# First layer's feed-forward output by seven block products in three passes; second layer's modulation multiplied by GpSimd and summed by ScalarE

## The chip, the cores and the metric

The kernel runs on one core of a Trainium2 chip. The profile names the engines PE (TensorE's matmuls), PEld (its weight loads), DVE (VectorE), ACT (ScalarE), POOL (GpSimd) and SP (SyncE, which here issues DMAs alone). The metric is the device time of one execution in microseconds, the median of several runs.

## The reference

Two passes of a two-layer transformer share all weights: 128 context tokens and 512 latent tokens, 640 columns in all, of model width 1024. Every sub-layer is modulated by a condition (shift, scale and gate, one set for the context tokens and one for the latent ones), and each layer ends with a SwiGLU feed-forward of inner width 2816:

```python
def ada_modulation(cond, w_mod, b_mod):
    m = jax.nn.silu(cond) @ w_mod + b_mod
    return jnp.split(m, 6, axis=-1)

def swiglu(h, w_in, w_out):
    gate, up = jnp.split(h @ w_in, 2, axis=-1)
    return (jax.nn.silu(gate) * up) @ w_out

for l in range(DEPTH):
    sh1_p, sc1_p, g1_p, sh2_p, sc2_p, g2_p = ada_modulation(cond_ctx, w_mod[l], b_mod[l])
    ...
    xp = xp + g1_p * out_p
    hp = modulate(rms_norm(xp, norm_ffn[l]), sh2_p, sc2_p)
    xp = xp + g2_p * swiglu(hp, w_ffn_in[l], w_ffn_out[l])
```

The latent tokens (xs, hs) go the same way. Layer 0's mixer is latent attention and neighbourhood attention, layer 1's is grouped-query attention. All is float32.

## The kernel before

Activations lie with features on the 128 partitions, as 8 tiles of 128x640, in two halves of 320 columns. A float32 product is made of three matmuls (`mm3`): weight and operand are each split into a rounded high part (ACT copies it) and a low part (DVE subtracts it from the source, "split" below), and high x high, high x low and low x high are added in PSUM.

*Feed-forward input.* The first three of 22 feature blocks are plain matmuls. The 19 others, the loop blocks, use a scheme with seven half-size products in place of eight for the 2x2 blocks (gate and up) x (left and right columns): DVE makes sums of the weights (`seven`: X and W are the raw weights, Y and Z are sums), ACT and DVE split them, and PE makes seven products of 12 matmuls into the banks fg, fd and fu, with operands named q, D, C, N, E. ACT copies partial results out of PSUM (p, u), DVE adds them (up, g), ACT applies silu, DVE multiplies (sg). Both layers do this alike.

*Feed-forward output.* In layer 1 (`ffn_out_seven`) it is a seven-product scheme as well: `hidden_pair` turns each pair of blocks into seven operands (a, D, N, b, c, C, E) split by ACT and DVE and spilled to DRAM by SP (all but two pairs of eleven); the output then goes over three passes of 3, 4 and 4 pairs, in each over 4 pairs of output tiles, and reloads the operands pass by pass. In layer 0 it is direct: `hidden` splits each block once (hd), and two chunks of 9 and 13 blocks are multiplied into 8 output tiles, two halves each (fo); `residual` adds them to x on DVE. After the second chunk comes the norm of layer 1 (fn0) and its first operands (h10); half of the last two tiles is held back so that PE has work meanwhile.

*Modulation.* Layer 0's is mostly made by matmuls at the start. The remaining 48 tiles, layer 0's last gate (G2) and layer 1's first five sets, are made by `mod_side`: SP loads a 128x1024 weight tile, and DVE multiplies it with the silu of either condition (a broadcast tile cb) and sums over the row, in one instruction with an accumulated output (junk). Four tiles go in layer 0's output projection (`mixer_out`), 44 in layer 0's feed-forward, at places set by a table of counts by block and tile. Layer 1's last set is made in layer 1 the same way.

*Order.* Each engine runs its instructions in one fixed order, written down when the program is built; `after(x, f)` places what f issues behind x. A tile name with `bufs` buffers makes a writer wait until the buffer's last reader is done.

Of the kernel before, what the change touches and what calls it, by code (L numbers as in the profile page):

```python
# [45 lines left out]
FO_ORDER = list(range(FB - 3, FB)) + list(range(FB - 3))  # L46
# [5 lines left out]
def body(ctx, tc, xT, vecs, crow, wm0, wm0g1, wm0g, wm1, wA, wNV, wNA, wMK, wMV, wOA, wGQ, wGK, wGV, wOC,  # L52
         wFI, wFO, wFO1, cckvT, ckrT, cnkT, cnv, cgkT, cgv, rpbp, tabM, tabK, tabG, maskN,
# [143 lines left out]
    class Norm:  # L197
# [6 lines left out]
        def add(self, x, i, last=False):  # L204
            c0, c1 = HALF[i]
            if last:
                sq = self.alone[i] = tp.tile([P, HT], F32, tag="u", bufs=7, name=f"{self.name}sql{i}")
                S.activation(sq, x[:, c0:c1], AF.Square)
            elif self.k[i] == 0:
                S.activation(self.acc[:, c0:c1], x[:, c0:c1], AF.Square)  # L210
            else:
                sq = tp.tile([P, HT], F32, tag="u", bufs=7, name=f"{self.name}sq{self.k[i]}{i}")
                S.activation(sq, x[:, c0:c1], AF.Square)
                V.tensor_add(self.acc[:, c0:c1], self.acc[:, c0:c1], sq)
            self.k[i] += 1

# [942 lines left out]
    def mixer_out(wsrc, os_, order, xin, ml, name, nxt, pre, beside=None, early=False, hold=None):  # L1159
# [5 lines left out]
        if True:  # L1165
# [4 lines left out]
            def evac(n, c, ps):  # L1170
# [3 lines left out]
                nrm.add(x[n], c, n == KT - 1)  # L1174
# [60 lines left out]
    STAY = 3  # L1235
    FIRST, SECOND = FO_ORDER[:9], FO_ORDER[9:]

# [4 lines left out]
    def ffn_open(l):  # L1242

        ph = ExitStack()
        fk = ph.enter_context(tc.tile_pool(name=f"fk{l}", bufs=1, reuse_waits="tile"))
        dr = ph.enter_context(tc.tile_pool(name=f"dr{l}", bufs=1, space=bass.MemoryType.DRAM))
        fs = ExitStack()
        if l == 0:
            hd = [[fk.tile([P, T], F32R, name=f"hd{l}_{i}{c}") for c in "hl"] for i in range(1)]
            fp = su = fs.enter_context(tc.tile_pool(name=f"fp{l}", bufs=1, reuse_waits="tile"))  # L1250

            def scratch(name):
                a = fk.tile([P, 2 * D], F32, tag="cb", bufs=1, name=name + "32a")
                d = [fp.tile([P, 1024], F32, tag="wr", bufs=2, name=f"{name}32d{i}") for i in range(2)]
                room = [t[:, j * HT:j * HT + HT] for t, n in ((a, 6), (d[0], 3), (d[1], 3)) for j in range(n)]
                room += [tp.tile([P, HT], F32, tag="u", bufs=7, name=f"{name}32u{i}") for i in range(4)]
                return room[:KT], room[KT:]
        else:
            hd = []
            fp = ph.enter_context(tc.tile_pool(name=f"fp{l}", bufs=1, reuse_waits="tile"))  # L1260
            su = fs.enter_context(tc.tile_pool(name=f"su{l}", bufs=1, reuse_waits="tile"))

            def scratch(name):

                left, right = {}, {}
                for at, where in (((0, 4), left), ((1, 5), left), ((0, 1), right), ((2, 6), left), ((3, 7), left), ((2, 3), right)):
                    t = fk.tile([P, T], F32, tag="o", bufs=7, name=f"{name}32{'rl'[where is left]}{at[0]}")
                    for k, c in zip(at, HALF):
                        where[k] = t[:, c[0]:c[1]]
                for k in range(4, KT):  # L1270
                    right[k] = tp.tile([P, HT], F32, tag="u", bufs=7, name=f"{name}32u{k}")
                return [left[k] for k in range(KT)], [right[k] for k in range(KT)]
        w = []

        def pre():
            for i in range(2):
                w.append(unit(wFI[l, 0, i], 1024, f"wgu{l}_{i}", pool=fp))
        return ph, fk, dr, hd, fs, fp, w, (su, scratch), pre

    def seven(ru, rg, name, fp, split):  # L1280
# [3 lines left out]
        wX = split(ru, f"wX{name}")  # L1284
        t = fp.tile([P, 2, 512], F32R, tag="w4", bufs=2, name=f"wW{name}")
        wW = t[:, 0, :m], t[:, 1, :m]
        S.activation(wW[0], rg[:, m:], AF.Copy)
        V.tensor_tensor(wW[1], rg[:, m:], f(wW[0]), ALU.subtract)
        s13 = fp.tile([P, 1024], F32, tag="ws", bufs=2, name=f"s13{name}")[:, :n]
        V.tensor_tensor(s13[:, :m], rg[:, :m], rg[:, m:], ALU.add)  # L1290
        V.tensor_tensor(s13[:, m:], ru[:, :m], rg[:, :m], ALU.add)
        wY = split(s13, f"wY{name}")
        s24 = fp.tile([P, 1024], F32, tag="ws", bufs=2, name=f"s24{name}")[:, :n]
        V.tensor_tensor(s24[:, :m], s13[:, m:], rg[:, m:], ALU.add)
        V.tensor_tensor(s24[:, m:], s24[:, :m], ru[:, m:], ALU.add)
        wZ = split(s24, f"wZ{name}")
        return wX, wW, wY, wZ

    def ffn_out_seven(x, nxt, opened, ops, spilt, split, close, last):

        ph, fk, dr, hd, fs, fp, *_ = opened
        ng = gs[0][0]
        V.tensor_scalar_mul(ng, mods[1][:, G2:G2 + 8, :], -1.0)
        raws = [0]

        def raw(n, c0, m, name):
# [3 lines left out]
            nc.sync.dma_start(t, wFO1[n, :, c0:c0 + m])  # L1310
# [10 lines left out]
        def result(n, c, src, sign, end):  # L1321

            o = HALF[c][0]
            for c0, c1, i in HCOND[c]:
                V.scalar_tensor_tensor(x[n][:, c0:c1], src[:, c0 - o:c1 - o],
                                       ng[:, n, i:i + 1] if sign < 0 else mods[1][:, G2 + n, i:i + 1], x[n][:, c0:c1], ALU.mult, ALU.add)
# [848 lines left out]
```

## Time and profile before

| | us |
|---|---|
| median of 3 runs | 1471.37 (1470.99 to 1471.61) |
| the profiled execution: time | 1473.53 |
| its span, first to last instruction | 1471.2 |
| PE busy in the span | 1438.7 |
| DVE busy | 1232.6 |
| ACT busy | 781.5 |
| POOL busy | 178.5 |

Layer 0's output projection (oa) runs from about 321 to 373 us, its feed-forward input to 655, the output to 809; layer 1's attention follows, its output projection (oc) from 992, its feed-forward input from 1077 and output from 1327 to the end. A row such as `700.00:750.00 50.00, 50.00 (x343)` reads: a stretch of 50 us in which PE was busy for 50.00 us with 343 instructions. A row of the timeline gives start, duration, engine, line, operation, output <- inputs, shape. One DVE operation often ends a little after the next has started.

### The profile page before, as it was taken

Reading aid. Unit: us, or ns where it says so; the run is one execution under the profiler, and the core shown is the slowest. Engines: PE = TensorE matmul, PEld = TensorE weight load, DVE = VectorE, ACT = ScalarE, POOL = GpSimd, SP = SyncE. Lnnn points to the kernel's source line nnn. Section 1 sums busy time; section 2 is a strip of 40 time slices with the busy share of each in tenths; the row PEclk is TensorE's granted clock in tenths of the full one; section 3 lists DMA queues with packets and bytes.
Section 4 is the critical chain, followed back from the end, with each engine's and each line's share of the span. In section 5 each row is a group of like instructions: output and inputs, shape, how many; then the busy total and the mean of one; then the engine's idle time right before and its main releaser. Section 6 shows DMA issues by size and latency. Waiting matters only on the chain.

```text
span 1471.2 us, 25849 instructions
## 1 busy us (share of the span) xinstructions
PE 1438.7 (98%) x9764; PEld 1391.0 (95%) x9764; DVE 1232.6 (84%) x2353; ACT 781.5 (53%) x1531; POOL 178.5 (12%) x276
## 2 busy tenths in 40 slices
PE   5999999999999999999999999999999999999997
PEld 3989979889999999999999999989999999999997
DVE  5877768977998888965997888888899898989976
ACT  5446657863755555531223666672656555555443
POOL 0046635520000000000000122220000000000000
PEclk9999999999999999999999999999999999999999
DMA  9653451125164555568764300115245555548572
GB/s 372 218 155 125 144 164 41 44 89 184 48 218 168 171 171 175 170 235 314 238 222 146 100 31 30 46 51 176 87 167 190 178 179 180 178 141 300 180 268 72
DMA packets 82724, 234.17 MB, mean 159 GB/s; under 512 B 9256, under 2 KB 15560, under 8 KB 82216
## 3 DMA queue, kind: packets, MB, share of 16 engines
q1 hardware_dynamic: 80240, 228.12, 46.2%
q10 hardware_dynamic: 1944, 3.48, 0.7%
q8 instruction: 76, 1.25, 0.3%
q0 software_dynamic: 416, 0.93, 0.2%
q14 instruction: 48, 0.39, 0.1%
HBM read 192.82 MB, written 36.66 MB: 156 GB/s over the span
## 4 chain that ended last, share of the span: by engine, by line
PE 88%; DVE 5%; ACT 3%; DMA 2%; issue 2%; SPq 0%; DVEq 0%; ACTq 0%
PE fg L64 21%; PE fd L64 9%; PE fgo L64 5%; PE fo L64 5%; PE fu L64 4%; PE gq L64 3%; PE fdo L64 2%; PE nk L64 2%; PE gs L64 2%; PE go L64 2%; PE nq L64 1%; PE fuo L64 1%; PE gt L68 1%; PE mod L64 1%; PE gvp L64 1%
## 5 line engine op out<-in xcount | busy, mean ns | idle before, releaser
L1742 DVE SCALAR_TENSOR_TENSOR junk<-wm,cb 128x1024 bf16<-128x1024 f32 x88 | 107.4, 1220 | 6.1 <-DMA wm<-in_wm 5.0
L64 PE MATMUL gq<-h10h,wgq 128*128 128x320 f32 x256 | 65.8, 316 | 0.0
L269 POOL TENSOR_SCALAR h10h<-h10t,gs,mods 128x320 fp32r<-128x320 f32 x4 | 3.9, 991 | 429.7 <-DVE h10t L263 423.7
L1482 ACT ACTIVATE wY<-s 128x1024 fp32r<-128x1024 f32 x38 | 40.3, 1061 | 26.8 <-PE fg L64 22.5
L2010 POOL TENSOR_TENSOR xr<-xw,fn1rs 128x320 f32<-128x320 f32 x2 | 1.7, 861 | 412.8 <-ACT fn1rs L237 412.8
L1482 ACT ACTIVATE wZ<-s 128x1024 fp32r<-128x1024 f32 x38 | 40.2, 1057 | 20.0 <-PE fd L64 15.2
L1483 DVE TENSOR_TENSOR wZ<-s,wZ 128x1024 fp32r<-128x1024 f32 x38 | 46.4, 1222 | 2.1
L1483 DVE TENSOR_TENSOR wY<-s,wY 128x1024 fp32r<-128x1024 f32 x38 | 46.4, 1220 | 0.3
L64 PEld LDWEIGHTS gq<-h10h,wgq 128*128 128x128 f32 x256 | 44.9, 189 | 0.6
L1591 DVE TENSOR_TENSOR sg<-up,sg 128x640 f32<-128x640 f32 x38 | 31.3, 824 | 15.7 <-ACT sg L1590 14.6
L1590 ACT ACTIVATE sg<-fg 128x320 f32<-128x320 f32 x38 | 16.7, 439 | 48.4 <-PE fg L64 48.4
L1612 ACT ACTIVATE p<-fd 128x320 f32<-128x320 f32 x38 | 16.6, 438 | 45.9 <-PE fd L64 45.8
L64 PE MATMUL gq<-h10l,wgq 128*128 128x320 f32 x128 | 39.4, 308 | 0.0
L1947 ACT ACTIVATE gp<-gs,gb,rq 128x640 f32<-128x640 f32 (+1 forms) x40 | 31.9, 796 | 13.2 <-DVE gb L1946 11.8
L64 PE MATMUL fg<-h01E,wW 128*128 128x320 f32 x228 | 36.6, 309 | 0.9 <-DVE g L1622 0.9
L64 PE MATMUL fg<-h11N,wZ 128*128 128x320 f32 x228 | 36.7, 309 | 0.0
L64 PE MATMUL fg<-h01q,wX 128*128 128x320 f32 x228 | 36.7, 309 | 0.0
L64 PE MATMUL fu<-h11q,wX 128*128 128x320 f32 x228 | 36.6, 309 | 0.0
L64 PE MATMUL fg<-h01N,wZ 128*128 128x320 f32 x228 | 36.6, 309 | 0.0
L64 PE MATMUL fd<-h01q,wZ 128*128 128x320 f32 x228 | 36.6, 309 | 0.0
L64 PE MATMUL fd<-h11q,wZ 128*128 128x320 f32 x228 | 36.6, 309 | 0.0
L64 PE MATMUL fg<-h11q,wX 128*128 128x320 f32 x228 | 36.5, 309 | 0.0
(3412 smaller groups left out, 5299.0 us busy)
## 6 DMA issues: line engine op xcount, KB each, us to landing
wm<-in_wm SPq DMA_DIRECT2D x48, 512.0 KB, 3.8
mraw<-in_wm SPq DMA_DIRECT2D x8, 1024.0 KB, 13.2
mraw<-in_wm SPq DMA_DIRECT2D x14, 512.0 KB, 3.9
wmv<-in_wm0g SPq DMA_DIRECT2D x8, 512.0 KB, 4.0
wm<-in_wm0g SPq DMA_DIRECT2D x8, 512.0 KB, 4.6
ruo<-in_wFO SPq DMA_DIRECT2D x8, 512.0 KB, 3.7
rgo<-in_wFO SPq DMA_DIRECT2D x8, 512.0 KB, 5.7
x<-in_xT SPq DMA_DIRECT2D x8, 320.0 KB, 5.3
```

The costliest lines, as they stand in the source:

```text
L64: cls.last = nc.tensor.matmul(*a, **k)
L68: cls.last = nc.tensor.transpose(*a, **k)
L269: G.tensor_scalar(h[:, c0:c1], t, self.gsl[:, k, 0:1], self.ml[:, self.sh + k, 0:1], ALU.mult, ALU.add)
L1482: S.activation(h, src, AF.Copy)
L1483: V.tensor_tensor(w_, src, f(h), ALU.subtract)
L1590: last = S.activation(sg[:, 0:HT], g[:, :HT], AF.Silu, scale=-1.0)
L1591: V.tensor_tensor(sg, up, sg, ALU.mult)
L1612: S.activation(p5, b5[:, :HT], AF.Copy)
L1742: V.scalar_tensor_tensor(junk, raw, 1.0, cb[:, c, :], ALU.mult, ALU.mult, accum_out=mods[l][:, j0 + i, c:c + 1])
L1947: gexp[h, j] = S.activation(dst, src, AF.Exp, bias=nb, scale=rq[:, j:j + 1], accum_out=ll[:, j:j + 1])
L2010: G.tensor_tensor(x[k][:, c0:c1], root[1][k], nrm.rs[:, c0:c1], ALU.mult)
```

## The change

1. Layer 0's feed-forward output takes layer 1's form: `hidden_pair` for both layers, `ffn_out_seven` with a layer argument, three passes, the weights in one tensor in the order of the passes. Its last two output tiles (e0, e1) have an order of their own in which results go from PSUM to x directly, and the next norm's calls stand between the last products.
2. 44 modulation tiles leave DVE and SP. A `Stream` makes them in 88 units of 128x512 (first all tiles' left halves, then the right ones): POOL loads a unit and multiplies it with the two conditions in two instructions (the second in place); ACT sums each product by a copy with an accumulated output ("add-up"). The right half's sum goes to a scratch column and is added at the end of a set. `pump(anchor, n)` advances it n slots behind an ACT instruction; a unit takes two slots, and the add-ups of a unit stand in the two slots after its multiplies. Slots: 26 at the squares of the output projection, 8 in layer 0's second and third block, 5 in each of its 19 loop blocks, 5 in each of the first ten output blocks: 179 for the 178 needed. The conditions come in halves of 512 as well.
3. `seven` hands its four parts out when first asked for, and layer 0 has fewer weight buffers (2 in place of 3; one for W).

```diff
-            def __init__(self, i, n, c0):
+            def __init__(self, i, n, c0, where=None, make="XWYZ"):
...
             def copy(self, what, ps):
                 t = self.held[what] = tp.tile([P, HT], F32, tag="u", bufs=7, name=f"{what}{self.name}")
-                S.activation(t, ps[:, :HT], AF.Copy)
+                pump(S.activation(t, ps[:, :HT], AF.Copy), 1 + 2 * (what == "u2"))
...
+        if l == 0:
+            pump(None, None)
+            e0 = Block(len(PASSES) - 1, 2, c0, (wp, fp, fp), "XYZ")
+            e0.p1()
+            e0.p2()
+            prev.p4()
+            e0.make("W")
+            e1 = Block(len(PASSES) - 1, 3, c0, (wp, wp, wp), "XYZ")
+            e1.p1()
+            e0.p6(True)
+            e1.p2()
+            e0.p7_direct()
+            e1.p6(True)
+            e0.p4()
+            e1.make("W")
+            e1.p7_direct()
+            e0.p5_direct()
+            e1.p4(True)
+            e1.p5_direct()
+            nxt(x, nrm, 0, range(3))
+            e0.p3_direct()
+            nxt(x, nrm, 0, range(3, 6))
+            e1.p3_direct()
+            nxt(x, nrm, 0, range(6, KT))
...
             product(g, wX, 0, 11, True)
-            S.activation(p1, g[:, :HT], AF.Copy)
+            pump(S.activation(p1, g[:, :HT], AF.Copy), 1)
...
-            for c in range(2):
-                junk = pool.tile([P, D], mybir.dt.bfloat16, tag="junk", bufs=1, name=f"junk{l}{j0 + i}{c}")
-                V.scalar_tensor_tensor(junk, raw, 1.0, cb[:, c, :], ALU.mult, ALU.mult,
-                                       accum_out=mods[l][:, j0 + i, c:c + 1])
...
+        def fetch(self, u):
+            if u < len(self.units):
+                h, l, src, j0, i = self.units[u]
+                t = self.raws[u] = self.pool.tile([P, 512], F32, tag="mr", bufs=3, name=f"wm{h}{l}_{j0 + i}")
+                G.dma_start(t, src[i][:, 512 * h:512 * h + 512])
+
+        def multiply(self, u):
...
+                t = self.pool.tile([P, 512], F32, tag="mt", bufs=2, name=f"mt{h}{l}_{j0 + i}")
+                G.tensor_tensor(t, self.raws[u], self.cb[:, 0, :], ALU.mult)
+                G.tensor_tensor(self.raws[u], self.raws[u], self.cb[:, 1, :], ALU.mult)
+                self.prods[u] = t, self.raws.pop(u)
+
+        def add_up(self, u, c, anchor):
...
+            t = self.prods[u][c]
+            m, at = (mods[1], G2 + i) if h else (mods[l], j0 + i)
+            after(anchor, lambda: S.activation(t, t, AF.Copy, accum_out=m[:, at, c:c + 1]))
...
+                if self.slot == 0:
+                    self.fetch(0)
+                    self.fetch(1)
+                self.add_up(u - 1, odd, anchor)
+                if odd:
+                    self.fetch(u + 2)
+                else:
+                    self.multiply(u)
+                self.slot += 1
```

The order on three engines at the places that matter. First ACT in layer 0's output projection, from the fifth output tile's weights (oaw) on; oansq are squares for the norm, mt and wm the two products of a unit. Before:

```order
L175 ACTIVATE oaw_4499<-oaw4r 128x1024
L210 ACTIVATE oanacc<-xr_4322 128x320 x2
L213 ACTIVATE oansq_4340<-xr_4336 128x320
L213 ACTIVATE oansq_4348<-xr_4336 128x320
L213 ACTIVATE oansq_4392<-xr_4388 128x320
L175 ACTIVATE oaw_4572<-oaw5r 128x1024
L213 ACTIVATE oansq_4421<-xr_4388 128x320
L213 ACTIVATE oansq_4465<-xr_4461 128x320
L175 ACTIVATE oaw_4610<-oaw6r 128x1024
```

And now:

```order
L1727 ACTIVATE mt_44_4337,mods_98<-mt_44_4337 128x512
L1727 ACTIVATE wm_44_4331,mods_98<-wm_44_4331 128x512
L212 ACTIVATE oansq_4362<-xr_4358 128x320
L1727 ACTIVATE mt_45_4349,mods_98<-mt_45_4349 128x512
L1727 ACTIVATE wm_45_4333,mods_98<-wm_45_4333 128x512
L212 ACTIVATE oansq_4377<-xr_4358 128x320
L1727 ACTIVATE mt_46_4366,mods_98<-mt_46_4366 128x512
L1727 ACTIVATE wm_46_4340,mods_98<-wm_46_4340 128x512
L212 ACTIVATE oansq_4428<-xr_4424 128x320
L1727 ACTIVATE mt_47_4381,mods_98<-mt_47_4381 128x512
L174 ACTIVATE oaw_4650<-oaw5r 128x1024
L1727 ACTIVATE wm_47_4353,mods_98<-wm_47_4353 128x512
```

Seven add-ups have come ahead of the split of oaw5; the splits of oaw6 and oaw7 stand behind 12 and 16.

Second, a loop block of layer 0: ACT from the split of wX for block 10 to the split of wZ (wX, wZ, wY, wW are weights, p and u copies out of PSUM, sg silu, hd the hidden block's high part). Before:

```order
L1482 ACTIVATE wX_10_6239<-wu_10r 128x1024
L1482 ACTIVATE wZ_10_6254<-s_10_6251 128x1024
L1482 ACTIVATE wY_10_6248<-s_10_6245 128x1024
L1623 ACTIVATE sg_8_5989<-g_8_5993 128x320
L1610 ACTIVATE p_9_6126<-fg_9_6121 128x320
L1612 ACTIVATE p_9_6127<-fd_9_6122 128x320
L1590 ACTIVATE sg_8_5989<-fg_8_5985 128x320
L1287 ACTIVATE wW_10_6242<-wg_10r 128x512
L1542 ACTIVATE hd_2h<-sg_8_5989 128x640
L1616 ACTIVATE u_9_6128<-fg_9_6121 128x320
L1482 ACTIVATE wX_11_6369<-wu_11r 128x1024
```

And now:

```order
L1538 ACTIVATE wX_10_6585<-wu_10r 128x1024
L1662 ACTIVATE sg_8_6280<-g_8_6284 128x320
L1727 ACTIVATE mt_26_6332,mods_99<-mt_26_6332 128x512
L1648 ACTIVATE p_9_6453<-fg_9_6448 128x320
L1727 ACTIVATE wm_26_6255,mods_99<-wm_26_6255 128x512
L1538 ACTIVATE wY_10_6591<-s_10_6588 128x1024
L1650 ACTIVATE p_9_6454<-fd_9_6449 128x320
L1727 ACTIVATE mt_27_6426,mods_99<-mt_27_6426 128x512
L1624 ACTIVATE sg_8_6280<-fg_8_6276 128x320
L1727 ACTIVATE wm_27_6316,mods_99<-wm_27_6316 128x512
L1282 ACTIVATE wW_9_6518<-wg_9r 128x512
L1564 ACTIVATE op4a<-sg_8_6280 128x320
```

Between the same copies and splits stand add-ups, one per slot; p and u are what frees PE's banks. POOL, which had no instruction from the end of the output projection to the end of layer 0, now has in the same block:

```order
L1709 DMA wm_26_6255<-in_wm 128x512
L1709 DMA wm_27_6316<-in_wm 128x512
L1717 TENSOR_TENSOR mt_26_6332<-wm_26_6255,cbs_4335 128x512
L1718 TENSOR_TENSOR wm_26_6255<-wm_26_6255,cbs_4335 128x512
L1717 TENSOR_TENSOR mt_27_6426<-wm_27_6316,cbs_4335 128x512
L1718 TENSOR_TENSOR wm_27_6316<-wm_27_6316,cbs_4335 128x512
L1709 DMA wm_28_6383<-in_wm 128x512
```

Third, PE at the end of layer 0, up to layer 1's first key product (gk). Before, the last of the held tiles' matmuls:

```order
L64 MATMUL fo_1_71_9314<-hr_17l,wo_1_71_9343 128x320
L64 MATMUL fo_1_71_9314<-hr_17h,wo_1_71_9343 128x320
L64 MATMUL fo_1_71_9314<-hr_18h,wo_1_71_9343 128x320
L64 MATMUL fo_1_71_9314<-hr_18l,wo_1_71_9343 128x320
L64 MATMUL fo_1_71_9314<-hr_18h,wo_1_71_9343 128x320
L64 MATMUL gk0a<-h10h_9407,wgk_9538 128x320
L64 MATMUL gk0a<-h10l_9415,wgk_9538 128x320
L64 MATMUL gk0a<-h10h_9407,wgk_9538 128x320
```

And now, from the norm's first matmul (fn0p) on:

```order
L63 MATMUL fn0p_10266<-fn0acc,ones 128x320
L63 MATMUL fdo_2_2_10215<-or4c,wZo_2_2_10033 128x320 x3
L63 MATMUL fdo_2_2_10215<-or5c,wZo_2_2_10033 128x320 x3
L63 MATMUL fdo_2_2_10215<-or6c,wZo_2_2_10033 128x320
L63 MATMUL fn0p_10266<-fn0sql_10246,ones 128x320
L63 MATMUL fdo_2_2_10215<-or6c,wZo_2_2_10033 128x320 x2
L63 MATMUL fdo_2_2_10215<-or7c,wZo_2_2_10033 128x320 x3
L63 MATMUL fdo_2_3_10248<-or4c,wZo_2_3_10104 128x320 x3
L63 MATMUL fdo_2_3_10248<-or5c,wZo_2_3_10104 128x320 x3
L63 MATMUL fdo_2_3_10248<-or6c,wZo_2_3_10104 128x320 x3
L63 MATMUL fdo_2_3_10248<-or7c,wZo_2_3_10104 128x320 x3
L63 MATMUL gk0a<-h10h_10271,wgk_10371 128x320
```

Behind the norm's second matmul stand 2 + 3 + 12 = 17 matmuls of the last products before gk0a; before the change 57 of the held halves stood behind the norm's.

434 lines of the change are left out of this document (183 added, 251 removed).

## The prediction

> **What bounds the kernel now.** I read the page's engine shares and slices first, then busy time by stage, then single instructions in order of time.
>
> ```profile
> span 1471.2 us, 25849 instructions
> ...
> PE 1438.7 (98%) x9764; PEld 1391.0 (95%) x9764; DVE 1232.6 (84%) x2353; ACT 781.5 (53%) x1531; POOL 178.5 (12%) x276
> ...
> DVE  5877768977998888965997888888899898989976
> ...
> POOL 0046635520000000000000122220000000000000
> ```
>
> PE is full, DVE is near full, and POOL does next to nothing from the tenth slice to the twenty-second, where layer 0's feed-forward runs. The busy times of that part, and of the same stages of layer 1, which already have the changed form (columns: us, then busy us of PE, PEld, DVE, ACT, POOL, clock, DMA share, GB/s):
>
> ```profile
> 321.00:365.00 44.00, 44.00 (x303) 44.00 (x302) 31.27 (x63) 14.37 (x23) 0.00 (x0) 1.00 0.65 219
> 476.96:526.22 49.26, 49.26 (x339) 49.26 (x338) 44.62 (x66) 25.89 (x40) 0.00 (x0) 1.00 0.52 177
> 700.00:750.00 50.00, 50.00 (x343) 50.00 (x342) 48.28 (x86) 11.42 (x15) 0.00 (x0) 1.00 0.72 234
> 1148.86:1198.12 49.26, 49.26 (x339) 49.26 (x338) 44.37 (x71) 28.77 (x50) 0.00 (x0) 1.00 0.56 180
> 1327.00:1371.00 44.00, 44.00 (x302) 43.98 (x301) 41.51 (x78) 23.11 (x37) 0.00 (x0) 1.00 0.86 309
> 1370.50:1419.74 49.24, 49.24 (x338) 49.24 (x338) 40.81 (x68) 20.79 (x29) 0.00 (x0) 1.00 0.67 234
> ```
>
> The rows are: layer 0's output projection; four of its feed-forward blocks; its feed-forward output; then four blocks of layer 1, its output in the pass of three pairs, and in a pass of four. PE waits for nothing anywhere, at clock 1.00. Fewer matmuls therefore shorten the span directly, as long as DVE stays under PE; it has 5 us in 49 to spare.
>
> **The change part by part.** *Matmuls.*
>
> ```profile
> 642.15 1.92 PE L64 MATMUL fg<-h01E,wW 128*128 128x320 f32 x12
> 643.91 1.92 PE L64 MATMUL fg<-h01N,wZ 128*128 128x320 f32 x12
> ```
>
> Twelve start every 1.76 us, 0.1467 each. Layer 0's output has 8 tiles x 22 blocks x 2 halves x 3 = 1056; seven products of 11 pairs, 4 tile pairs and 3 make 924. So 132 x 0.1467 = **-19.3 us**, if PE still sets the pace.
>
> *DVE's modulation* goes:
>
> ```profile
> L1742 DVE SCALAR_TENSOR_TENSOR junk<-wm,cb 128x1024 bf16<-128x1024 f32 x88 | 107.4, 1220 | 6.1 <-DMA wm<-in_wm 5.0
> ```
>
> That is 107 us of DVE, but PE did not wait for it, so nothing by itself. In return layer 0 gets layer 1's pair operands, weight sums and splits. Its stages then cost DVE what the layer 1 rows show: 44.37 / 4 = 11.1 us in a block whose matmuls take 12.3. The extra spills and reloads (63 tiles each way for 38) lie under the DMA shares of those same rows: no cost.
>
> *GpSimd's multiplies* are what is new: 176 tensor-by-tensor products of 128x512 and 88 loads of 256 KB on POOL.
>
> ```profile
> L952 POOL TENSOR_TENSOR mql<-mqt,mqh 128x320 fp32r<-128x320 f32 x16 | 14.3, 895 | 21.5 <-ACT mqh L951 21.5
> L176 POOL TENSOR_TENSOR wm<-wm0r,wm 128x768 fp32r<-128x768 f32 x1 | 1.8, 1838 | 0.0
> L749 POOL DMA_DIRECT2D out_o_nkT<-nkf x4 | 2.3, 586 | 3.0 <-ACT nkf L748 2.9 <-issue 0.2
> ```
>
> Between 0.895 at 320 and 1.838 at 768, a 512 takes 1.30 us; issuing a load takes 0.6. A loop block has 5 slots, so 5 multiplies: 6.5 us and 1.5 of issuing, which POOL alone could do in 12.3. But POOL is not alone:
>
> ```profile
> 836.65 1.22 DVE L176 TENSOR_TENSOR wgq<-wgq1r,wgq 128x1024 fp32r<-128x1024 f32 x1
> ...
> 947.33 0.96 POOL L397 TENSOR_SCALAR gp<-gp,gr_3r 128x640 f32<-128x640 f32 x1 [2.68 <-DVE gr_3r L396]
> ...
> 947.61 1.75 DVE L176 TENSOR_TENSOR wgq<-wgq7r,wgq 128x1024 fp32r<-128x1024 f32 x1
> ...
> 950.53 1.85 POOL L397 TENSOR_SCALAR gp<-gp,gr_4r 128x128 f32<-128x128 f32 x1 [2.24 <-DVE gr_4r L396]
> ...
> 950.55 1.21 DVE L176 TENSOR_TENSOR ocw<-ocw0r,ocw 128x1024 fp32r<-128x1024 f32 x1
> 951.68 0.54 DVE L1811 SCALAR_TENSOR_TENSOR gqr<-gqc,vec,tg 128x320 f32<-128x320 f32 x1
> ...
> 245.20 1.98 POOL L852 TENSOR_TENSOR wm<-wm2r,wm 128x384 fp32r<-128x384 f32 x2
> ...
> 246.71 0.42 DVE L407 TENSOR_TENSOR mpp0ptl<-ms,mpp0pth 128x256 fp32r<-128x256 f32 x1
> ```
>
> The same DVE split takes 1.22 alone and 1.75 where POOL was busy when it started: it ends at 949.36, 1.07 after POOL's 948.29. Only its start-up passes meanwhile. Three us later POOL's small operation lasts 1.85 and ends at 952.38, behind one DVE operation and into the next. So the two exclude each other when DVE reads two SBUF operands. A DVE operation with one operand in PSUM (ms) ran through POOL's at its usual 0.42. A multiply thus costs DVE about 1.30 - 0.15 = 1.15 us, unless it falls on a PSUM operation or idle DVE. Nearly all that DVE does here (splits, sums, operands) reads two SBUF operands.
>
> [...]
>
> *A loop block.* DVE has three operations with PSUM input, 0.4 us from start to start:
>
> ```profile
> 1160.79 0.49 DVE L1618 TENSOR_TENSOR up<-fu,p 128x320 f32<-128x320 f32 x1
> 1161.22 0.49 DVE L1620 TENSOR_TENSOR up<-fd,u 128x320 f32<-128x320 f32 x1
> 1161.63 0.48 DVE L1510 TENSOR_TENSOR op3E<-n,op3E 128x320 fp32r<-128x320 f32 x1
> ```
>
> So 11.1 + 5 x 1.15 - 1.2 = 15.65 us. I add 0.5 (an estimate) for waits on ACT: behind an add-up that waits for a multiply stand the copies p and u, for which PE waits with its banks, silu, and the next split, for which DVE waits. That makes 16.15 against 12.31, +3.84, x 19 blocks = **+73**. Below: if only the data time counts (1.07 us for 1024 elements, 8032 SBUF elements a block, 8.4 us), 8.4 + 5.75 = 14.1, +34 in all. Above: every multiply and its add-up one behind the other with DVE, 11.1 + 6.5 + 5 x 0.82 = 21.7, +178. The add-up's 0.82 is from the nearest rows:
>
> ```profile
> L1287 ACT ACTIVATE wWo<-rgo 128x512 fp32r<-128x512 f32 x8 | 5.0, 626 | 4.7 <-PE fgo L64 3.3 <-DMA or6b<-sp6b 1.4
> L1069 ACT ACTIVATION_READ_ACCUMULATOR mp<-ms,mn 128x1 f32 x32 | 6.3, 196 | 0.0
> ```
>
> *The output.* In a pass of four pairs DVE has 40.81 / 4 = 10.2; with 5.75, less four PSUM operations (1.6), plus 0.5, that is 14.85 against 12.31: +2.54 x 6 blocks = 15. In the pass of three, 41.51 x 9.23 / 44 = 8.7, so 13.35 against 9.23: +4.1 x 4 = 16.5. **+32**. Below, by data time (6592 and 5184 elements), 12.6 and 11.2 a block: 10 in all; above, one behind the other, 20.8 and 19.3: 91.
>
> *The output projection* carries 13 units (26 multiplies), and ACT's squares and weight splits stand behind their add-ups.
>
> ```profile
> 332.88 0.82 ACT L210 ACTIVATE oanacc<-xr 128x320 f32<-128x320 f32 x2
> ...
> 353.01 1.06 ACT L175 ACTIVATE oaw<-oaw7r 128x1024 fp32r<-128x1024 f32 x1 [2.42 <-PE oa4b L64]
> ...
> 359.97 3.52 PE oa L64 x24
> ...
> 366.13 1.08 PE oanp L64 x4
> ```
>
> The first load follows the first square (332.9), so multiplies begin near 338.5. The split of oaw7 stands behind the add-up of the eighth unit: 8 x (2.6 + 0.6) = 25.6, then add-up and split, 368 at the earliest for weights that PE takes at 359.97 today: 8 us late. With DVE busy 31 of 44 us I add 0.6 us a multiply: 18 late. The square for the norm at 366 stands behind the eleventh unit and is later still, with PE's held halves to cover part; on POOL the four copies that make h01q stand behind the fourteenth unit's multiplies. **+18** (6 to 30). Layer 0's first three blocks carry 8 multiplies beside a full DVE: 9.2 us, half in gaps, **+5** (0 to 9).
>
> *The end of layer 0* loses cover:
>
> ```profile
> 800.32 0.70 PE L64 MATMUL fn0p<-fn0acc,ones 128*128 128x320 f32 x2
> ...
> 809.20 0.31 PE L64 MATMUL gk0a<-h10h,wgk 128*128 128x320 f32 x1
> ...
> 813.49 0.48 DVE L272 TENSOR_TENSOR h10l<-h10f,h10h 128x320 fp32r<-128x320 f32 x1
> ```
>
> Now 8.2 us of matmuls lie between the norm and gk0a; in the changed order it is 17 matmuls, 2.5 us. DVE makes the eight operands until 813.97, 13 us after the norm; PE would be through gk in 2.5 + 7. **+3** (0 to 8).
>
> Sum: -19.3 + 73 + 32 + 18 + 5 + 3 = +112. On the profiled execution's 1473.5 us (span 1471.2 and 2.3 around it) that is 1585; the median of the runs is 2.1 lower, 1471.4, so **1583 us**.
>
> **The rivals.** *Perfect interleaving* (0.18): only data times add. 34 + 10 + 6 - 19.3 = +31, **1502**. For: POOL's waits can fall into DVE's start-ups. Against: 1.75 for 1.22 shows whole waits.
>
> *Serial hand-over* (0.16): DVE passes POOL over as at 950.53, ACT stands at the add-up, the next split is late, and DVE idles. 178 + 91 + 30 + 9 + 8 - 19.3 = +297, **1768** at worst, and over 1640 if half of it comes true. It decides once a multiply is regularly later than its slot.
>
> *Covered* (0.06): the multiplies fit where DVE is idle or on PSUM operations, and PE keeps the pace: 1471.4 - 19.3 + 3 = **1455**. [...] Had the change not removed the matmuls, this would be 0 instead of -19; the program's order has the 924. About 0.02 for a balance within 0.2%.
>
> **How the numbers follow.** The forecast has 0.58, from 1530 to 1640. The range runs from the perfect interleaving's 1502, rounded down to 1500, into half the serial case, 1665; what is left out is the covered case and the serial case's far end, under 0.2. Within 0.2% (3 us, about what a measurement can tell) 0.02; faster 0.06; slower 0.92.
>
> **What would show it.** Right: DVE busy near 9.5 tenths and PE with gaps in layer 0's feed-forward, a loop block near 16 us, DVE splits of 1.22 lengthened towards 2 and multiplies over 1.3 there, and PE waiting for DVE or ACT at fg and fd. The output near 800 (before) would take longer, not 19 us less. Layer 1's times should not move. Wrong: blocks of 12.3 us with multiplies of 1.3 beside splits of 1.22. If the multiplies are undisturbed but ACT waits long at the add-ups, the serial case is the one.

## Result and profile after

| | us |
|---|---|
| before, median of 4 runs | 1471.49 (1470.99 to 1472.95) |
| changed, median of 4 runs | 1603.05 (1599.68 to 1610.23) |
| ratio, 95% interval | 1.0899 (1.0858 to 1.0940) |
| the profiled execution of the changed kernel: time, span | 1605.37, 1603.6 |

The change makes the kernel 9% slower. 1583 was predicted, with a range from 1500 to 1665. The page of the changed kernel, with the lines that answer those of before (engine shares; the span in 40 slices; the stream's groups):

```profile
span 1603.6 us, 26525 instructions
...
PE 1469.1 (92%) x9634; PEld 1400.0 (87%) x9634; DVE 1370.8 (85%) x2412; ACT 926.5 (58%) x1988; POOL 514.5 (32%) x542
...
DVE  5868679876999999999777978789789998988977
...
POOL 0057546475356665566555211222000000000000
PEclk9999999998999999999898999999999999999999
...
L1717 POOL TENSOR_TENSOR mt<-wm,cbs 128x512 f32<-128x512 f32 x88 | 147.7, 1678 | 229.8 <-DMA wm<-in_wm 126.1
L1718 POOL TENSOR_TENSOR wm<-wm,cbs 128x512 f32<-128x512 f32 x88 | 140.1, 1593 | 6.3
...
L1727 ACT ACTIVATE mt<-mt 128x512 f32<-128x512 f32 x88 | 54.9, 624 | 57.5 <-POOL mt L1717 55.7
```

PE has 130 records of matmuls fewer and yet its share falls from 98% to 92%: it now waits. POOL has its work from the third slice to the twenty-second in place of the third to the ninth, and DVE stands at 9 from the eleventh to the nineteenth, the loop. The same shows in busy times by stage: the 19 loop blocks of layer 0, its output, and four blocks of layer 1, which the change does not touch.

```profile
444.00:752.00 308.00, 258.51 (x1606) 249.87 (x1605) 297.94 (x343) 188.77 (x433) 184.40 (x144) 0.95 0.53 175
752.00:935.00 183.00, 149.46 (x920) 143.36 (x919) 145.42 (x228) 91.70 (x198) 83.29 (x70) 0.91 0.57 199
1280.00:1330.00 50.00, 50.00 (x343) 50.00 (x342) 45.04 (x72) 29.53 (x51) 0.00 (x0) 1.00 0.54 180
```

In the loop DVE is busy for 297.94 of 308 us, and PE for 258.51. In the output neither is full (145 and 149 of 183): there something else is late. Layer 1 runs as before.

The stages, each from its first matmul to the next stage's, as the timeline of PE shows them, for both kernels and for the experiments below. (The output projection's first matmul, at 311.0 in the kernel before, stands among the last of the attention's. The loop and the output are divided where the loop's last product ends. gk is layer 1's key product, up to the last matmul of the keys' norm.)

| kernel | output projection | first three blocks | 19 loop blocks | output | gk | whole, median |
|---|---|---|---|---|---|---|
| before | 64.0 | 44.0 | 236.3 | 153.9 | 25.5 | 1471.49 |
| changed | 79.8 | 56.5 | 308.3 | 182.7 | 30.6 | 1603.05 |
| form alone | 64.0 | 43.9 | 235.2 | 135.1 | 30.7 | 1455.41 |
| no multiplies | 66.3 | 43.9 | 235.2 | 139.5 | 30.6 | 1459.20 |
| no add-ups | 94.2 | 141.1 | 297.7 | 135.0 | 30.6 | 1644.53 |
| no loads | 76.9 | 52.1 | 308.0 | 164.0 | 30.6 | 1578.76 |
| small add-ups | 78.0 | 58.7 | 303.3 | 176.6 | 30.6 | 1597.45 |
| narrow multiplies | 66.7 | 52.2 | 236.6 | 145.5 | 30.6 | 1479.99 |
| summed on DVE | 73.2 | 49.8 | 257.0 | 160.4 | 30.7 | 1515.18 |
| two places on DVE | 75.8 | 51.2 | 236.5 | 143.8 | 30.6 | 1540.57 |

**How DVE is slowed.** The timeline of a loop block of the changed kernel (start, duration, engine, line, operation), POOL and DVE alone, where DVE has four short operations in a row:

```profile
567.50 1.43 POOL L1718 TENSOR_TENSOR wm<-wm,cbs 128x512 f32<-128x512 f32 x1
...
567.69 1.58 DVE L1565 TENSOR_TENSOR op4b<-sg,op4b 128x320 fp32r<-128x320 f32 x1
...
568.89 1.53 POOL L1717 TENSOR_TENSOR mt<-wm,cbs 128x512 f32<-128x512 f32 x1
...
569.20 1.58 DVE L1565 TENSOR_TENSOR op4c<-sg,op4c 128x320 fp32r<-128x320 f32 x1
...
570.50 1.43 POOL L1718 TENSOR_TENSOR wm<-wm,cbs 128x512 f32<-128x512 f32 x1
...
570.70 1.58 DVE L1565 TENSOR_TENSOR op4C<-c,op4C 128x320 fp32r<-128x320 f32 x1
...
574.14 0.48 DVE L1565 TENSOR_TENSOR op4E<-n,op4E 128x320 fp32r<-128x320 f32 x1
```

The same kind of split takes 1.58 with a multiply of POOL about it and 0.48 (op4E) without: in these rows DVE and POOL take turns, one instruction each. A DVE operation with an operand in PSUM does not take part here:

```profile
494.80 2.15 POOL L1718 TENSOR_TENSOR wm<-wm,cbs 128x512 f32<-128x512 f32 x1
495.73 0.48 DVE L1661 TENSOR_TENSOR g<-fg,p 128x320 f32<-128x320 f32 x1
496.13 1.90 DVE L1539 TENSOR_TENSOR wX<-wu_7r,wX 128x1024 fp32r<-128x1024 f32 x1
```

g (fg is in PSUM) runs at its usual 0.48 inside a multiply; the split of wX behind it needs 1.90 and waits the multiply out, which ends at 496.95. It is no single case: of DVE's sums with an operand in PSUM (L1357, L1657, L1659, L1661) 31 overlap a multiply, and none takes more than 0.49 us.

**Who waits.** Waits in the changed kernel's loop, and then in its output (engine, tile and line that waited, who released it: us, times, longest):

```profile
PE fg L63 <- DVE g L1661: 34.4, 17, 3.7
...
PE fg L63 <- ACT u L1655: 12.6, 11, 1.8
...
ACT mt L1727 <- POOL mt L1717: 5.7, 3, 3.4
```

```profile
POOL mt L1717 <- DMA wm<-in_wm: 58.3, 16, 6.4
ACT mt L1727 <- POOL mt L1717: 43.2, 16, 7.7
...
PE fgo L63 <- DVE p5o L1357: 12.0, 6, 6.3
```

In the loop PE waits for DVE's last sum g of the block before, 2.0 us a time on average: DVE is late, and ACT hardly ever stands at an add-up. In the output ACT does, for 43 us, and the chain begins at POOL's loads. The timeline shows the worst case:

```profile
772.50 1.11 POOL L1709 DMA_DIRECT2D wm<-in_wm  x2
...
779.75 1.26 POOL L1717 TENSOR_TENSOR mt<-wm,cbs 128x512 f32<-128x512 f32 x1 [6.14 <-DMA wm<-in_wm]
781.04 0.63 ACT L1727 ACTIVATE mt<-mt 128x512 f32<-128x512 f32 x1 [7.73 <-POOL mt L1717]
...
783.14 0.42 ACT L1353 ACTIVATE p1o<-fgo 128x320 f32<-128x320 f32 x1
...
783.61 0.90 PE L63 MATMUL fgo<-op9N,wZo 128*128 128x320 f32 x2 [7.21 <-ACT p1o L1353]
```

The row at 772.50 issues two loads, the multiply can start at 779.75, the add-up at 781.04; behind that add-up in ACT's order stand the copies for two splits and the copy p1o, which frees the bank fgo for PE. From 776.40 (783.61 less the 7.21 that PE waited) to 779.75 none of the four engines worked, while the DMA engines were busy for 0.95 of that time: the loads came late among other transfers, 7.25 us after the row of their issue, where the median from issue to landing is 3.6.

### The profile page after: what moved, and what is told of

Its sections match the earlier page's. It is cut to its first block, busy times and chain, and to the rows that moved or that the text cites. A ratio compares the mean times of both kernels' runs of the same rounds, so it can differ in the third digit from the quotient of the medians.

```text
span 1603.6 us, 26525 instructions
## 1 busy us (share of the span) xinstructions
PE 1469.1 (92%) x9634; PEld 1400.0 (87%) x9634; DVE 1370.8 (85%) x2412; ACT 926.5 (58%) x1988; POOL 514.5 (32%) x542
## 5 line engine op out<-in xcount | busy, mean ns | idle before, releaser
L1717 POOL TENSOR_TENSOR mt<-wm,cbs 128x512 f32<-128x512 f32 x88 | 147.7, 1678 | 229.8 <-DMA wm<-in_wm 126.1
L1718 POOL TENSOR_TENSOR wm<-wm,cbs 128x512 f32<-128x512 f32 x88 | 140.1, 1593 | 6.3
L1727 ACT ACTIVATE mt<-mt 128x512 f32<-128x512 f32 x88 | 54.9, 624 | 57.5 <-POOL mt L1717 55.7
L63 PEld LDWEIGHTS fg<-h01E,wW 128*128 128x128 f32 x228 | 42.5, 234 | 38.8 <-DVE g L1661 38.8
L1727 ACT ACTIVATE wm<-wm 128x512 f32<-128x512 f32 x88 | 54.8, 623 | 14.3 <-POOL wm L1718 14.3
L63 PE MATMUL fg<-h01C,wY 128*128 128x320 f32 x228 | 38.5, 318 | 12.8 <-ACT u L1655 12.6
L63 PEld LDWEIGHTS fg<-h01C,wY 128*128 128x128 f32 x228 | 34.2, 190 | 15.9 <-ACT u L1655 15.9
L1709 POOL DMA_DIRECT2D wm<-in_wm x80 | 45.7, 572 | 7.1 <-ACT wm L1727 7.1
L1689 DVE SCALAR_TENSOR_TENSOR junk<-wm,cb 128x1024 bf16<-128x1024 f32 (+1 forms) x24 | 33.9, 1410 | 10.2 <-DMA wm<-in_wm0g 5.9
L63 PEld LDWEIGHTS fg<-h01N,wZ 128*128 128x128 f32 x228 | 38.5, 210 | 1.3 <-ACT p L1648 1.3
```

Source lines behind the costliest of these rows:

```text
L63: cls.last = nc.tensor.matmul(*a, **k)
L1689: V.scalar_tensor_tensor(junk(f"junk{l}{j0 + i}{c}"), raw, 1.0, box[0][:, c, :], ALU.mult, ALU.mult, accum_out=mods[l][:, j0 + i, c:c + 1])
L1709: G.dma_start(t, src[i][:, 512 * h:512 * h + 512])
L1717: G.tensor_tensor(t, self.raws[u], self.cb[:, 0, :], ALU.mult)
L1718: G.tensor_tensor(self.raws[u], self.raws[u], self.cb[:, 1, :], ALU.mult)
L1727: after(anchor, lambda: S.activation(t, t, AF.Copy, accum_out=m[:, at, c:c + 1]))
```

## Experiments

The theory, called port theory in the expectations: a multiply of GpSimd takes its time out of DVE, because the two take turns as in the rows above (1.58 us for a split of 0.48), and DVE is the bound wherever POOL works. "Port" is only the author's name for these turns: what lies behind them no run shows. Its rivals: the seven-product form itself, ScalarE's extra load, and waits handed on in order (late loads, then add-ups, then copies). Each experiment is the changed kernel with one edit, unless it says otherwise.

### Form alone

```diff
+            V.memset(mods[1][:, :, :], 0.0)
...
-                t = self.raws[u] = self.pool.tile([P, 512], F32, tag="mr", ...)
-                G.dma_start(t, src[i][:, 512 * h:512 * h + 512])
...
-                G.tensor_tensor(t, self.raws[u], self.cb[:, 0, :], ALU.mult)
-                G.tensor_tensor(self.raws[u], self.raws[u], self.cb[:, 1, :], ALU.mult)
...
-            after(anchor, lambda: S.activation(t, t, AF.Copy, accum_out=m[:, at, c:c + 1]))
...
```

> The changed kernel without its stream: no loads, multiplies or add-ups for the 44 modulation tiles, whose columns are set to zero. Port theory (a GpSimd multiply takes its time from a full DVE): the form by itself keeps PE's pace, a loop block takes 12.3 us as in layer 1, and the whole 1473.5 - 19.3 + 3 (the end of layer 0) = 1455 to 1460 us. Rival, the form itself (fewer weight buffers, the parts of a weight made later): blocks stay above 14 us and the whole above 1500.

Measured: 1455.41 us (1454.98 to 1455.48), ratio to before 0.9873 (0.9851 to 0.9895). Its loop and its output, in the same columns as above:

```profile
415.00:650.00 235.00, 235.00 (x1605) 235.00 (x1604) 208.18 (x335) 135.81 (x237) 0.00 (x0) 1.00 0.50 171
650.00:785.00 135.00, 135.00 (x919) 134.58 (x918) 118.74 (x217) 63.62 (x101) 0.18 (x1) 1.00 0.65 224
```

PE is never idle in them, at clock 1.00. This kernel is 16 us faster than the first runs of the kernel before (1471.49) and 18 faster than those taken beside it (1473.73); some 2 us of that are the modulation that it leaves out, by the run without it below, and the rest is the form's. The stream costs all of 1603.05 - 1455.41 = 147.6 us, 0.84 for each of 176 multiplies. DVE's busy time in the loop shows how: 208.18 here and 297.94 with the stream. In those 308 us POOL has 144 instructions, of which 48 issue loads and 96 are multiplies: the 90 us are 0.93 us of DVE for each.

### No multiplies

```diff
...
-                G.tensor_tensor(t, self.raws[u], self.cb[:, 0, :], ALU.mult)
-                G.tensor_tensor(self.raws[u], self.raws[u], self.cb[:, 1, :], ALU.mult)
-                self.prods[u] = t, self.raws.pop(u)
+                self.prods[u] = (self.raws.pop(u),) * 2
```

> The changed kernel without its 176 GpSimd multiplies: the loads stay, and ScalarE sums the raw weights, twice, at the same places. Port theory: the loop blocks fall from 16.2 to about 12.5 us and the whole to 1455 to 1480, what remains being add-ups that wait for late loads. Rival, ScalarE's own load (176 add-ups of 0.82 us in its order): blocks stay near 16 us and the whole above 1560. Rival, late loads: the loop falls, but the output keeps its waits of some 30 us, so about 1490.

Measured: 1459.20 us (1456.73 to 1461.08), ratio 0.9899 (0.9876 to 0.9921).

```profile
418.00:653.00 235.00, 235.00 (x1605) 235.00 (x1604) 209.66 (x340) 187.74 (x431) 25.77 (x48) 1.00 0.69 225
```

The loads are there, and ACT has its 52 us more than in the form alone, but PE is full. Loads and add-ups by themselves cost 4 us. ScalarE's load is no cause by itself, and neither is lateness of loads while nothing else is slow.

### No add-ups, and small ones

The products are not summed, and the 44 tiles' columns are zero, in both of these runs.

```diff
+            V.memset(mods[1][:, :, :], 0.0)
...
-            after(anchor, lambda: S.activation(t, t, AF.Copy, accum_out=m[:, at, c:c + 1]))
```

> The changed kernel without the 176 add-ups on ScalarE: loads and multiplies stay, the products are not summed and the 44 tiles' columns are set to zero. Port theory: the loop blocks stay near 15.7 us (only the 0.5 for ScalarE's waits goes), the output loses the waits behind the add-ups, some 20 to 30 us, and the whole is 1565 to 1585. Rival, hand-over through ScalarE's order or its load: blocks fall to 12.5 us and the whole below 1490.

Measured: 1644.53 us (1642.36 to 1646.00), ratio 1.1156 (1.1133 to 1.1179): slower than with the add-ups, against every expectation. The table shows where: the first three blocks take 141 us, and the output, where nothing is left of the stream, 135.0.

```profile
403.00:544.00 141.00, 63.88 (x294) 57.24 (x294) 140.15 (x94) 31.77 (x64) 131.25 (x127) 0.67 0.33 105
```

POOL is busy for 131 of 141 us. The add-ups had paced it (shown by the next run): a product's buffer, and so the next multiply, had waited for ACT's place in the program. Without them POOL runs on, and DVE gets one instruction in between, here one of 0.48 us every 1.50:

```profile
482.97 0.48 DVE L329 TENSOR_TENSOR h01C<-h0132u,h01C 128x320 fp32r<-128x320 f32 x1
483.37 0.48 DVE L329 TENSOR_TENSOR h01E<-h0132l,h01E 128x320 fp32r<-128x320 f32 x1
...
485.29 1.58 DVE L1565 TENSOR_TENSOR op0a<-sg,op0a 128x320 fp32r<-128x320 f32 x1
...
486.79 1.58 DVE L324 TENSOR_TENSOR h0132l<-h0132l,h0132r 128x320 f32<-128x320 f32 x1
488.30 1.58 DVE L1577 TENSOR_TENSOR sg<-sg 128x320 f32<-128x320 f32 x1
...
494.08 1.27 POOL L1719 TENSOR_TENSOR mt<-wm,cbs 128x512 f32<-128x512 f32 x1
```

Undisturbed, DVE starts such an operation every 0.40 us (the first two rows); here every 1.50. That is the price without any cover: 1.10 us of DVE for a multiply of 1.27. Over the whole kernel it is (1644.53 - 1455.41) / 176 = 1.07, with PE's lower clock (0.67 in the row above) in it.

If this reading is right, an add-up that keeps the place but does next to nothing must bring the old picture back:

```diff
-            after(anchor, lambda: S.activation(t, t, AF.Copy, accum_out=m[:, at, c:c + 1]))
+            after(anchor, lambda: S.activation(t[:, 0:1], t[:, 0:1], AF.Copy))
```

> The changed kernel with each add-up cut to a copy of one column (about 0.2 us; nothing is summed, the 44 tiles' columns are set to zero): GpSimd's products are still waited for by ScalarE at the same places, so the stream keeps its pace, but ScalarE's load is gone. Port theory: the loop blocks stay at 15.5 to 16.2 us and the whole at 1585 to 1603, unlike the kernel without add-ups, in which GpSimd ran ahead unpaced and took 1644. Rival, ScalarE's 144 us of summing are what slows: below 1540.

Measured: 1597.45 us (1593.82 to 1602.01), ratio 1.0843 (1.0813 to 1.0873), with a loop of 303.3. So the pace returns, and the summing itself is worth about 6 us. The miss of the run before was one of the experiment, which took away two things (ACT's load and POOL's pace), and not of the price.

### No loads

```diff
-                t = self.raws[u] = self.pool.tile([P, 512], F32, tag="mr", bufs=3, ...)
-                G.dma_start(t, src[i][:, 512 * h:512 * h + 512])
+                if u == 0:
+                    self.raw = self.pool.tile([P, 512], F32, tag="mr", bufs=1, name="wm_once")
+                    G.dma_start(self.raw, src[i][:, 512 * h:512 * h + 512])
...
+                self.prods[u] = [self.pool.tile([P, 512], F32, tag="mt", bufs=4, ...) for c in range(2)]
+                for c in range(2):
+                    G.tensor_tensor(self.prods[u][c], self.raw, self.cb[:, c, :], ALU.mult)
```

> The changed kernel with one loaded unit in place of 88: every multiply reads that one, with both products in four buffers of their own, so no multiply waits for a load. Port theory: the loop blocks stay at 16 us; in the output GpSimd's 58 us of waits for loads and ScalarE's 43 us of waits for multiplies go, which gives back 20 to 30 us: 1573 to 1583. Rival, late loads as the main cause: the whole falls below 1500.

Measured: 1578.76 us (1577.35 to 1579.35), ratio 1.0709 (1.0689 to 1.0730). The loop stays at 308.0; the output falls from 182.7 to 164.0.

```profile
746.00:910.00 164.00, 145.65 (x918) 140.91 (x917) 153.62 (x226) 90.77 (x198) 72.35 (x46) 0.95 0.54 185
```

Now DVE is the fuller engine there too (153.62 of 164). Late loads are worth 18.7 us in the output and 24 in all; in the loop they are covered, though POOL waits for them there as well (63.8 us). With the loads their issuing has gone from POOL too (0.57 us each); the two were not told apart.

### Narrow multiplies

```diff
-                G.tensor_tensor(t, self.raws[u], self.cb[:, 0, :], ALU.mult)
+                G.tensor_tensor(t[:, 0:64], self.raws[u][:, 0:64], self.cb[:, 0, 0:64], ALU.mult)
```

The second multiply and the add-ups likewise.

> The changed kernel with every GpSimd multiply and every add-up cut to 64 of its 512 columns (the other columns are neither multiplied nor summed); loads, order and the number of instructions stay. Port theory, price by duration: a multiply of some 0.35 us costs VectorE 0.1 to 0.3, loop blocks 12.3 to 12.7 us, the output keeps only the small waits that remain without multiplies: 1458 to 1475 us. Rival, a price by instruction (each one makes VectorE wait for about the same time whatever its size): blocks stay near 15 us and the whole above 1560.

Measured: 1479.99 us (1477.20 to 1486.71), ratio 1.0055 (1.0037 to 1.0073).

```profile
L1717 POOL TENSOR_TENSOR mt<-wm,cbs 128x64 f32<-128x64 f32 x88 | 53.1, 604 | 293.8 <-DMA wm<-in_wm 184.6 <-ACT mt L1727 53.8 <-ACT wY L1538 15.1
```

The same number of instructions at the same places leaves the loop at 236.6:

```profile
427.00:663.00 236.00, 235.17 (x1603) 234.64 (x1602) 215.00 (x340) 156.57 (x431) 83.25 (x143) 1.00 0.66 226
```

DVE's busy time there grows by 215.00 - 208.18 = 6.8 us over the form alone, 0.07 for a multiply of 0.60 in place of 0.93 for one of 1.68. So here the price goes by duration and not by the instruction; over the whole kernel it is (1479.99 - 1459.20) / 176 = 0.12 us each. The 5 us over what was expected lie in the first three blocks (52.2) and the output (145.5). DVE is full in neither (46.5 and 120.0 us busy). In the first blocks PE waits once 3.3 us for a sum of the norm on DVE and once 2.4 us for h01q, whose copies POOL has behind the stream; the rest was not taken apart.

### Summed on DVE

Nothing is left out here: DVE multiplies and sums each unit at the stream's slots (both in the unit's own two slots, where ACT's add-ups had stood two slots later).

```diff
-                G.tensor_tensor(t, self.raws[u], self.cb[:, 0, :], ALU.mult)
-                G.tensor_tensor(self.raws[u], self.raws[u], self.cb[:, 1, :], ALU.mult)
...
-            after(anchor, lambda: S.activation(t, t, AF.Copy, accum_out=m[:, at, c:c + 1]))
...
+            V.scalar_tensor_tensor(junk, self.prods[u], 1.0, self.cb[:, c, :], ALU.mult, ALU.mult, accum_out=m[:, at, c:c + 1])
...
-                self.add_up(u - 1, odd, anchor)
...
+                self.add_up(u, odd, anchor)
...
```

> The changed kernel with its stream's loads and places kept, but each unit multiplied and summed by VectorE in one instruction per condition (128x512, about 0.69 us each by the 0.69 of a 128x512 sum of weights in the form alone) in place of a GpSimd multiply and a ScalarE add-up. Port theory: VectorE now does the whole work itself and yet is less full than beside GpSimd, 11.1 + 5 x 0.69 = 14.55 us a loop block instead of 16.2; 1455 + 43 for the loop, 4 and 3 for the first blocks and the output projection, 20 for the output: about 1525 (1505 to 1545). Rival, GpSimd really takes work off VectorE: 1600 or more.

Measured: 1515.18 us (1512.56 to 1517.51), ratio 1.0283 (1.0265 to 1.0300), 88 us faster than the changed kernel. The group, and the loop:

```profile
L1724 DVE SCALAR_TENSOR_TENSOR mj<-wm,cbs 128x512 bf16<-128x512 f32 x176 | 120.2, 683 | 2.6 <-DMA cbs<-crs 2.4
...
L1724 DVE DVE_READ_ACCUMULATOR mj<-wm,cbs 128x1 f32 x176 | 14.3, 81 | 0.0
```

```profile
430.00:687.00 257.00, 245.54 (x1603) 234.85 (x1602) 253.75 (x518) 130.14 (x235) 25.53 (x47) 1.00 0.61 205
```

DVE does multiply and sum in 0.68 us itself, and 0.08 to read the sum out, where a multiply of POOL, without the sum, keeps it waiting for 1.10. By DVE's busy time in the loop, the measure that gave 0.93, the 92 that run there cost (253.75 - 208.18) / 92 = 0.50 each. The move to GpSimd took nothing off DVE; it gave it more. (The loop cost 22 us and not the 43 expected, chiefly because 0.69 a product had been put for what adds 0.50 to DVE's busy time. Why it adds less than its own 0.68 was not shown.)

### Before, without its modulation

```diff
...
-            raw = raw_(src[i], f"wm{l}_{j0 + i}")
-            for c in range(2):
-                ...
+            if pool is not skip[0] or l == 0 and i < 4 or j0 == G2 and l:
+                raw = raw_(src[i], f"wm{l}_{j0 + i}")
+                ...
```

> The kernel before without VectorE's 80 modulation instructions of layer 0's feed-forward and their loads (40 tiles, whose columns are set to zero); the direct output stays. If PE is the bound and VectorE's 107 us cost nothing there: 1468 to 1472 us, no faster than the kernel before. Rival, they cost PE something: below 1465.

Measured: 1469.57 us (1467.68 to 1471.78), ratio 0.9982 (0.9973 to 0.9992). The work that the change set out to take from DVE (40 of its 44 tiles are left out here) had cost the kernel before 2 us.

### Two places on DVE

A try at a version faster than both: the seven-product form, with modulation as whole instructions of DVE (128x1024), two in each loop block, eight in the output projection, two in the output's blocks of four pairs, and the last two sets in layer 1's attention.

```diff
-                if pump and (c == 0 or n < 5):
-                    pump(sq, 2)
+                if pump and 1 <= n < 5:
+                    pump(sq, 1)
...
-            pump(S.activation(p1, g[:, :HT], AF.Copy), 1)
+            S.activation(p1, g[:, :HT], AF.Copy)
...
+    late = Late([(1, wm1[j:j + 8], j) for j in (SH2, SC2)])
...
```

> The seven-product form with all of the 44 tiles' modulation on VectorE (128x1024 and, in layer 1, 128x512 at a time), put where the form alone and the version on VectorE showed room: 8 instructions in the output projection, 2 in each of 19 loop blocks, 2 in a block of the output's passes of four pairs, and the last two sets (16 tiles) in layer 1's attention. Theory (the change's form is worth 16 us and the modulation costs what VectorE can't fit beside PE): the version with 5 x 0.76 = 3.8 us in a loop block lost 1.1 to 1.2 us a block, so 2 x 1.30 = 2.6 fit; 8 in the output projection fit in the 10 us it absorbed; layer 1's attention has about 25 us of room for 64 x 0.76 = 49 us. So 1455 + 0 to 25: 1460 to 1480, likeliest 1470, no clear gain on the kernel before. Rival, the order of VectorE's instructions and not its room decides: 1490 or more.

Measured: 1540.57 us (1535.14 to 1541.87), ratio 1.0462 (1.0445 to 1.0478): a miss. The loop, and layer 1's attention, which takes 151 us in the form alone:

```profile
434.40:670.90 236.50, 235.28 (x1603) 234.71 (x1602) 232.40 (x388) 131.46 (x236) 7.40 (x14) 1.00 0.60 201
845.00:1039.00 194.00, 168.45 (x1023) 156.38 (x1021) 161.96 (x405) 99.97 (x230) 42.88 (x43) 0.88 0.22 69
```

```profile
L1717 DVE SCALAR_TENSOR_TENSOR mj<-wm,cbm 128x1024 bf16<-128x1024 f32 x28 | 34.2, 1223 | 2.3 <-DMA wm<-in_wm 2.2
```

The group is that of the loop alone: 28 of the instructions run there (the others of its 38 already before it, with 13 in place of 8 in the output projection, which takes 11.8 us longer than in the form alone; the first three blocks take 7.3 longer). Those 28 cost 1.3 us: in the loop they fit beside PE. In the attention the plan failed by 43 us with DVE busy for only 162 of 194. PE waits there most for the weights wgq:

```profile
PE gq L63 <- ACT wgq L174: 12.3, 6, 2.1
```

Room in DVE's average was not room at the places where the work was put. These 64 instructions also take their weights through the three buffers that wgq uses; which of the two made wgq late was not tried. No version that makes all of the modulation and is faster than before was found.

## Why the prediction was right, point by point

*What bounds.* DVE has little to spare in layer 0's feed-forward and becomes the bound: shown. It is busy for 9.7 tenths of the loop (297.94 / 308), and PE waits for its g.

*Matmuls, -19.3.* With the stream gone the output is 153.9 - 135.1 = 18.8 us shorter, at clock 1.00.

*Price of a multiply.* 1.15 us of DVE, from a split of 1.22 that took 1.75 in the kernel before. Measured 1.10 without cover. The 1.30 us for a 128x512 was 1.27. The exclusive turns and the exception for PSUM operands, read off single rows of before, hold in the changed kernel: 1.58 and 1.90 us beside a multiply with all operands in SBUF, 0.48 with one in PSUM. (POOL's small operation there ends at 952.38, after both DVE rows shown and not within the second, which ends at 952.22; the conclusion stands.)

That a multiply of 1.27 keeps DVE for only 1.10, because a start-up of DVE's operation passes meanwhile, is the prediction's reading, and was not tried by itself. The size fits: 0.48 us for 320 columns and 1.22 for 1024 leave, by a straight line through the two (an estimate), 0.14 that does not go with the columns, and 0.15 was taken off.

*Loop, +73.* Measured +72.0 (308.3 against 236.3); a block takes 16.2 us, as put. This term carried the prediction, and its parts hold too: 4.55 net of PSUM operations had been put for DVE's loss in a block, and it is 90 / 19 = 4.7. The 0.5 for waits on ACT is what DVE stands idle in a block (10 us in 19), but only about half of that is ACT's (4.9 us in all); 3.9 us are waits for weights to land. That size was luck in part.

*Output, +32.* Mis-sized: +48 (182.7 against 153.9 - 19.3). The term had been made from DVE's load and 0.5 us a block for ACT; late loads were in no part of it. Without loads the stage takes 164.0, or +29. The 19 us above that go with the loads: they come late, and ACT's order hands that on to PE, a piece of the rival "serial hand-over", seen in this stage.

*Output projection, +18; first three blocks, +5; end of layer 0, +3.* Measured +15.8, +12.5 and +5.1. The first came out by luck: all 18 had been put on the weights oaw7, and PE never waits for those. Its waits there are 4.9 us for the weights of the fourth to sixth tiles, 4.1 for the norm and 2.2 for x, and its busy time grows by 4.7 us (68.65 against 63.96), at a mean clock of 0.96. The last is the form's, since the form alone has it (30.7 against 25.5). The second was mis-sized: with multiplies of 64 columns it is still +8, so more than DVE's turns with POOL is in it, and it was settled only in part what.

*Sum.* 20 us above the predicted time: 16 from the output, 7.5 from the first three blocks, 2 from the end of layer 0, less 2 in the projection, 1 in the loop, and 3 by which the projection starts earlier (308.0 against 311.0), which was not forecast. So the total is near because its largest term, the loop, was right, and not because errors made each other good.

*The rivals.* Perfect interleaving (1502) falls to the alternation of 1.58 and 0.48. Covered (1455) is the time of the form alone, and so what the change would have given had the multiplies cost nothing; but five to a block would have had to fit into 12.3 - 11.1 = 1.2 us of idle time and 1.2 of PSUM operations, 0.5 each, and they took 0.93. Serial hand-over (1768) needs multiplies that are regularly later than their slot; in the loop they were not (ACT's 5.7 us). Half of its +297 would give 1620, not over 1640 as the prediction has it, and so the 1665 at the end of the range is not half of that case either.

*What would show it.* Splits beside a multiply took 1.90, as said, but many met none: the mean of wY's is 1.33, and the multiplies (1.68 and 1.59 on average) do as much of the waiting. PE waited at fg as said, hardly at fd.

## What to carry to other kernels

Before work is moved to GpSimd, see whether VectorE is full there and whether both read SBUF: in this kernel they then took turns (1.58 us for a split of 0.48), and in its loop a 128x512 product on GpSimd added 0.93 us to VectorE's busy time, against 0.50 for product and sum of its own. An average with room in it says little about a place; a stream beside a full engine is priced by what it takes from that engine, stage by stage. And where a consumer paces a producer, taking away the consumer is no test of the consumer alone.

## What the runs showed of the hardware that was not expected

*PE's clock.* The sum was made at clock 1.00. In the changed kernel, PE's rows and two stretches (the clock is the third number from the end) in a loop block:

```profile
575.48 3.51 PE L63 MATMUL fg<-h01E,wW 128*128 128x320 f32 x12 [2.70 <-DVE g L1661]
578.82 1.92 PE L63 MATMUL fg<-h01N,wZ 128*128 128x320 f32 x12
```

```profile
575.40:578.30 2.90, 2.82 (x10) 2.83 (x11) 2.90 (x4) 2.02 (x6) 1.67 (x1) 0.50 0.37 140
578.30:582.00 3.70, 3.70 (x25) 3.70 (x25) 3.63 (x4) 3.12 (x8) 2.15 (x2) 0.93 0.17 52
```

After a wait of 2.70 us the clock is 0.50 for some 3 us, and twelve matmuls take 3.51 us in place of 1.92. The stage's mean is 0.95 in the loop and 0.91 in the output, and 0.67 in the first blocks without add-ups. What this costs by itself was not separated: in the loop DVE is the later engine anyway, and as it stands idle for only 10 of 308 us, no more than that can come of the clock there.

The changed kernel's record of the clock shows more. Between 300 and 960 us it changes only in steps of 3.41 us (a stretch at 0.50 lasts 3.41, 6.83 or 10.24), and each of the 17 falls to 0.50 there follows a step in which PE was busy for at most 1.61 us (from 571.96 to 575.37, just before the rows above, 0.81), while no step with 1.73 us or more led to one. Each of the 17 steps has a wait of 1.80 us or more in it, or a part of one; the shortest is that from 708.95 to 710.75. The 1.61 holds for these stages alone: in layer 1's attention a fall, at 995.21, follows a step with 2.89 us (991.80 to 995.21) and two waits of 0.26.

*A VectorE operation with one tensor operand can be held too.* In the kernel without add-ups:

```profile
436.73 1.50 POOL L1720 TENSOR_TENSOR wm<-wm,cbs 128x512 f32<-128x512 f32 x1
...
437.04 1.28 DVE L305 TENSOR_SCALAR h0132r<-h01t,gs,mods 128x128 f32<-128x128 f32 x1
```

And one of the same form in the kernel with narrow multiplies, with no multiply near:

```profile
394.74 0.34 DVE L305 TENSOR_SCALAR h0132u<-h01t,gs,mods 128x128 f32<-128x128 f32 x1
```

Beside the multiply it takes 1.28 us in place of 0.34. It has one tensor in SBUF and two columns of scalars, so DVE was held without two tensor operands of its own as well; what else plays a part was not tried.
